# Three blocks of queries projected with tokens in rows and turned by VectorE and DMA, in a two-layer trunk on one Trainium2 core

## The chip, the cores and the metric

The kernel runs on one core of a Trainium2 chip. The metric is device time in microseconds of one execution. Three runs of the kernel before took 975.09, 975.46 and 979.18 us, median 975.46. A profile of one further execution is the source of all durations below. The engines are named as the profile names them: PE is TensorE (matmuls; PEld its weight loads), DVE is VectorE, ACT is ScalarE, POOL is GpSimd, SP is SyncE, which here only issues DMAs.

## The reference, cut to what matters

Two layers, each `h = h + Mixer(RMSNorm(h))`, on 256 tokens with 2048 features. Layer one is a gated DeltaNet with 16 heads of 128; layer two is attention over bands of chunks and takes no part in the change.

```python
def gated_deltanet(h, w_in, conv_w, a_log, dt_bias, out_norm_w, w_out):
    proj = h @ w_in                                # 2048 -> 8224 columns
    qkv = proj[..., :3 * A_INNER]                  # q: columns 0..2047, k, v
    z = proj[..., 3 * A_INNER:4 * A_INNER]
    ...
    qkv = jax.nn.silu(causal_depthwise_conv(qkv, conv_w))   # 4 taps along the tokens
    q = l2_norm(q) * (A_HEAD_DIM ** -0.5)
    k = l2_norm(k)
    ...                                            # decays, triangular solve, scan over 4 chunks
    o = rms_norm(o, out_norm_w) * silu(z)
    return o @ w_out
```

## The kernel before, in words

**Weights and products.** The weights come in a fixed plan of chunks of 512 KB, eight to a block of 512 columns. Each chunk is loaded on SP's queue (L178, tile wt, four buffers), rounded by a ScalarE cast (L204, tile whi) and its rest taken by a VectorE subtract (L205, tile wlo); whi and wlo have three buffers each. Three chunks are fetched ahead of the one in use. The input tokens are split in the same way (tile xb, a high and a low half), and a product is made of three: high by high, high by low, low by high. All big products are matmuls of line L257.

**Three ways to make a block of 512 columns.** "features": features in rows, weights as the stationary side, tokens streamed. "half": the same in halves of 256 columns, in which a weight's high part takes 512 streamed columns (both halves of xb side by side) and its low part 256. Two halves are joined: `joined` copies one part of the accumulator with ScalarE (L327, tile ev, two buffers) and adds the other with VectorE (L328); `scaled` then multiplies by the norm of each token on VectorE (L343, tile raw, one buffer). "tokens": tokens in rows, xb stationary and weights streamed, 96 matmuls of 512 columns. The accumulators of all of them are two buffers of PSUM (tile psp); small products use others (pss). In layer one the first q block is "features", q's other three, k and v are pairs of halves, and the gate z is "tokens".

**Convolution.** `conv` works with features in rows, since the taps shift along the tokens: for each of four groups of 128 features one ScalarE multiply (L546) and three VectorE multiply-adds (L548, tile cv). `q_rest` follows with Silu (L570), Square (L573), two transposes (L579) and a sum (L581); after the last block a small matmul (L587) makes the statistics of all heads.

**What sets the order.** While TensorE goes through a block, `tick` calls `step`, which advances one of several lanes of small work: a lane `landing` first, then bgq and bg2 in turn. q's and k's steps are in bgq in the order of the blocks, the decays of all heads (`decays`, three exponentials per head, L535, one head per chunk from chunk 33 on) in bg2. A lane whose step has to wait for something gives way and nothing behind it in the lane runs. The joining of halves goes ahead of all lanes (`now`). A scheduler then places each engine's instructions in one queue per engine; an instruction that waits holds all behind it on its engine.

**Turning a block by DMA.** Later parts of the kernel already turn tokens-in-rows blocks: `turn_tokens` transposes 32 x 32 squares on VectorE (L438), `trip` stores the tile to DRAM on POOL's queue (L418) and `back` loads it in another order with four DMAs on SP's queue (L424).

Of the kernel before, what the change touches and what calls it, by code (L numbers as in the profile page):

```python
# [10 lines left out]
AF = mybir.ActivationFunctionType  # L11
# [28 lines left out]
def tile_hybrid_trunk(  # L40
# [29 lines left out]
    def slot(tag, kb, dt=F32):  # L70

        return big.tile([P, kb * 256], dt, name=tag, tag=tag)
# [54 lines left out]
    def wide(w, col, c0=0, c1=CPB):  # L127
        return [(w, col, c, 512) for c in range(c0, c1)]
# [4 lines left out]
    def halves(w, col, n):  # L133
        return [x for j in range(n) for x in half(w, col + 256 * j)]


    plan = wide(a_w_in, 0) + halves(a_w_in, 512, 14)
    for col in (6144, 6656, 7168):
        plan += wide(a_w_in, col)
    plan += halves(a_w_in, 4096, 8) + wide(a_w_in, 7680)  # L140
# [198 lines left out]
    def scaled(dst, src, r):  # L339

        if isinstance(src, list):
            for i, ev in enumerate(src):
                dve.tensor_tensor(out=dst[:, 2 * i:2 * i + 2], in0=ev, in1=r.unsqueeze(1).broadcast_to([P, 2, T]),  # L343
                                  op=ALU.mult)
        else:
            dve.tensor_tensor(out=dst, in0=src, in1=r.unsqueeze(1).broadcast_to([P, 4, T]), op=ALU.mult)
# [192 lines left out]
    def conv(src, i0):  # L539

        raw = wk("raw", 1)
        scaled(raw, src, scales["x"][1])
        cv = wk("cv")
        yield cv
        for i in range(4):
            act.activation(out=cv[:, i, :], in_=raw[:, i, :], func=AF.Copy, scale=conv_w(i0 + i, 3))  # L546
            for s in (1, 2, 3):
                dve.scalar_tensor_tensor(out=cv[:, i, s:], in0=raw[:, i, :T - s], scalar=conv_w(i0 + i, 3 - s),  # L548
                                         in1=cv[:, i, s:], op0=ALU.mult, op1=ALU.add)
            yield cv  # L550
# [10 lines left out]
    def q_conv(gi, ps):  # L561
        for cv in conv(ps, 4 * gi):
            yield 1
        qmem[gi] = cv

    def q_rest(gi):
        if gi == 0:
            qmem["q"] = slot("g", 32)[:, :H * T].rearrange("p (h t) -> p h t", h=H)
        q = qmem["q"][:, 4 * gi:4 * gi + 4, :]
        act.activation(out=q, in_=qmem[gi], func=AF.Silu)  # L570
        yield 1
        sq = qmem[gi]
        act.activation(out=sq, in_=q, func=AF.Square)  # L573
        turn = dl[:, 4 * gi:4 * gi + 4, 0, 0:T]
        part = parts[:, 32 * gi:32 * gi + 32]
        yield 1
        for p in range(2):
            hs = slice(2 * p, 2 * p + 2)
            dve.transpose(out=turn[:, hs], in_=sq[:, hs])  # L579
            yield 1  # L580
        dve.reduce_sum(out=part.rearrange("p (h b) -> p h b", h=4), in_=turn.rearrange("p h (b d) -> p h b d", d=32),  # L581
                       axis=AX.X)
        yield 1
        if gi == 3:
            ps = ps_small()
            for c in range(4):
                pe.matmul(ps[32 * c:32 * c + 32, 0:32], lhsT=fold, rhs=parts[:, c:128:4], start=True, stop=True,  # L587
                          tile_position=(0, 32 * c))
            dve.tensor_copy(out=ssq, in_=ps[:, 0:32].rearrange("p (h t) -> p h t", t=2))
            yield 1  # L590
# [370 lines left out]
    for gi in range(4):  # L961
        if gi == 0:
            bgq.append(x_stats())
        ps = pair(xb, 2) if gi else block("features", xb, pre=x_split)
        bgq.append(q_conv(gi, ps))
        if gi == 0:
            bg2.append(decays())
        else:
            if gi == 1:
                bgq.append(q_rest(0))  # L970
            bgq.append(q_rest(gi))
    for gi in range(4):
        bgq.append(k_small(gi, pair(xb)))
    bgq.append(inversion())
# [397 lines left out]
```

## Time and profile before

| what | value |
|---|---|
| median of three runs | 975.46 us (975.09 to 979.18) |
| the profiled execution, its own time | 975.5 us |
| its span, first to last instruction | 973.6 us |
| TensorE busy, share of the span | 966.7 us, 99% |
| VectorE busy | 701.9 us, 72% |
| ScalarE busy | 517.2 us, 53% |
| granted TensorE clock, mean | 1.000 |

A busy time is the time in which an engine works on at least one instruction. In the rows that follow, "out<-in" are the names of the tiles, a size like 128x512 is partitions by elements, and behind "[" or the last "|" stands how long the engine was idle just before and what released it.

### The profile page before, as it was taken

Reading aid. Unit: us, or ns where it says so; the run is one execution under the profiler, and the core shown is the slowest. Engines: PE = TensorE matmul, PEld = TensorE weight load, DVE = VectorE, ACT = ScalarE, POOL = GpSimd, SP = SyncE. Lnnn points to the kernel's source line nnn. Section 1 sums busy time; section 2 is a strip of 40 time slices with the busy share of each in tenths; the row PEclk is TensorE's granted clock in tenths of the full one; section 3 lists DMA queues with packets and bytes.
Section 4 is the critical chain, followed back from the end, with each engine's and each line's share of the span. In section 5 each row is a group of like instructions: output and inputs, shape, how many; then the busy total and the mean of one; then the engine's idle time right before and its main releaser. Section 6 shows DMA issues by size and latency. Waiting matters only on the chain.

```text
span 973.6 us, 14322 instructions
## 1 busy us (share of the span) xinstructions
PE 966.7 (99%) x5291; PEld 821.7 (84%) x5291; DVE 701.9 (72%) x1143; ACT 517.2 (53%) x727; POOL 92.0 (9%) x128
## 2 busy tenths in 40 slices
PE   8999999999999999999999999999999999999998
PEld 7988888888888889888878888888888888888887
DVE  7789787998989877866586655566767676655464
ACT  8465887655547556544365544445454545444332
POOL 1001100122000000101000110111212120000000
PEclk9999999999999999999999999999999999999999
DMA  9657765645665665566978798788798986665695
GB/s 297 195 162 234 233 196 160 179 126 184 173 196 151 180 208 162 169 192 192 304 246 243 223 289 282 215 250 259 235 283 247 278 251 205 202 192 171 206 290 168
DMA packets 142277, 210.01 MB, mean 216 GB/s; under 512 B 10480, under 2 KB 80000, under 8 KB 142208
## 3 DMA queue, kind: packets, MB, share of 16 engines
q1 hardware_dynamic: 136208, 187.33, 64.7%
q0 software_dynamic: 5712, 21.52, 6.1%
q8 instruction: 41, 0.67, 0.3%
q14 instruction: 28, 0.23, 0.1%
q10 hardware_dynamic: 288, 0.26, 0.1%
HBM read 191.76 MB, written 17.32 MB: 215 GB/s over the span
## 4 chain that ended last, share of the span: by engine, by line
PE 93%; DMA 3%; ACT 1%; issue 1%; DVE 1%; SPq 0%; POOL 0%; ACTq 0%; POOLq 0%
PE psp L257 84%; PE pss L631 2%; PE pss L257 1%; PE pss L876 1%; DMA cv<-trip 1%; DMA trip<-cv 1%; PE pss L1159 1%; PE pss L1228 1%; DMA wt<-in_a_w_in_dram 1%; DMA wt<-in_a_w_out_dram 1%; ACT whi L204 0%; DVE wlo L205 0%; PE pss L897 0%; PE pss L898 0%; PE pss L899 0%
## 5 line engine op out<-in xcount | busy, mean ns | idle before, releaser
L205 DVE TENSOR_TENSOR wlo<-wt,whi 128x1024 fp32r<-128x1024 f32 (+2 forms) x324 | 390.0, 1207 | 208.4 <-ACT whi L204 205.0
L204 ACT CAST whi<-wt 128x1024 fp32r<-128x1024 f32 (+2 forms) x324 | 336.5, 1040 | 371.6 <-PE psp L257 288.9
L257 PE MATMUL psp<-whi,xb 128*128 128x512 f32 x1280 | 402.1, 392 | 0.0
L257 PEld LDWEIGHTS psp<-whi,xb 128*128 128x128 f32 x1280 | 240.0, 188 | 49.3
L257 PE MATMUL psp<-wlo,xb 128*128 128x512 f32 x640 | 249.8, 390 | 0.0
L257 PE MATMUL psp<-xb,whi 128*128 128x512 f32 (+1 forms) x832 | 196.2, 376 | 0.9 <-ACT whi L204 0.9
L257 PEld LDWEIGHTS psp<-xb,whi 128*128 128x128 f32 x832 | 148.2, 189 | 25.6 <-ACT whi L204 1.3
L257 PEld LDWEIGHTS psp<-wlo,xb 128*128 128x128 f32 x640 | 120.2, 188 | 24.5
L257 PE MATMUL psp<-whi,g 128*128 128x512 f32 x448 | 138.9, 390 | 0.0
L257 PE MATMUL psp<-xb,wlo 128*128 128x256 f32 x768 | 113.4, 285 | 0.7 <-DVE wlo L205 0.7
L257 PEld LDWEIGHTS psp<-xb,wlo 128*128 128x128 f32 x768 | 103.4, 191 | 5.3 <-DVE wlo L205 1.4
L257 PEld LDWEIGHTS psp<-whi,g 128*128 128x128 f32 x448 | 84.1, 188 | 17.3
L257 PE MATMUL psp<-wlo,g 128*128 128x512 f32 x224 | 87.9, 392 | 0.6 <-DVE wlo L205 0.6
L548 DVE SCALAR_TENSOR_TENSOR cv<-raw,sm,cv 128x255 f32<-128x255 f32 (+2 forms) x144 | 64.2, 479 | 2.4 <-ACT cv L546 2.0
L257 PEld LDWEIGHTS psp<-wlo,g 128*128 128x128 f32 x224 | 42.1, 188 | 10.3 <-DVE wlo L205 2.0
L546 ACT ACTIVATE cv<-raw,sm 128x256 f32<-128x256 f32 x48 | 22.2, 501 | 18.1 <-DVE raw L343 18.1
L418 POOL DMA_DIRECT2D trip<-cv x19 | 10.9, 571 | 190.8 <-DVE cv L438 160.6
L1172 ACT ACTIVATE raw<-raw,mx 128x128 f32<-128x128 f32 (+1 forms) x32 | 14.4, 449 | 16.8 <-DVE mx L1170 16.7
L1115 POOL TENSOR_SCALAR ssn<-ssn,uh 128x4 f32<-128x4 f32 x16 | 12.1, 767 | 68.2 <-DVE ssn L1113 68.2
L635 DVE TENSOR_TENSOR dl<-pss,dl 128x512 f32<-128x512 f32 (+1 forms) x32 | 16.4, 546 | 1.7 <-PE pss L631 1.7
L343 DVE TENSOR_TENSOR raw<-ev,rB 128x512 f32<-128x512 f32 x22 | 14.8, 684 | 2.8 <-DMA trip<-raw 2.8
L328 DVE TENSOR_TENSOR ev<-psp,ev 128x512 f32<-128x512 f32 x23 | 15.7, 682 | 0.1
(247 smaller groups left out, 746.0 us busy)
## 6 DMA issues: line engine op xcount, KB each, us to landing
wt<-in_b_w_in_dram SPq DMA_DIRECT2D x128, 512.0 KB, 4.4
wt<-in_a_w_in_dram SPq DMA_DIRECT2D x125, 512.0 KB, 4.0
wt<-in_a_w_out_dram SPq DMA_DIRECT2D x32, 512.0 KB, 5.2
wt<-in_b_w_out_dram SPq DMA_DIRECT2D x32, 512.0 KB, 4.1
trip<-cv POOLq DMA_DIRECT2D x19, 512.0 KB, 5.5
cv<-trip SPq DMA_DIRECT2D x60, 128.0 KB, 4.5
trip<-dl POOLq DMA_DIRECT2D x8, 384.0 KB, 4.4
tt<-line POOLq DMA_DIRECT2D x4, 512.0 KB, 8.3
```

The costliest lines, as they stand in the source:

```text
L204: cast = act.copy(out=hi[:, js, cs], in_=wt[:, js, cs])
L205: rest = dve.tensor_tensor(out=lo[:, js, cs], in0=wt[:, js, cs], in1=hi[:, js, cs].bitcast(F32), op=ALU.subtract)
L257: state["mm"] = pe.matmul(*args, **kw).ins
L328: dve.tensor_tensor(out=ev, in0=ps[:, :, 0, :], in1=ev, op=ALU.add)
L343: dve.tensor_tensor(out=dst[:, 2 * i:2 * i + 2], in0=ev, in1=r.unsqueeze(1).broadcast_to([P, 2, T]), op=ALU.mult)
L418: nc.gpsimd.dma_start(out=m, in_=u.rearrange("p x c j -> p c (x j)"))
L546: act.activation(out=cv[:, i, :], in_=raw[:, i, :], func=AF.Copy, scale=conv_w(i0 + i, 3))
L548: dve.scalar_tensor_tensor(out=cv[:, i, s:], in0=raw[:, i, :T - s], scalar=conv_w(i0 + i, 3 - s), in1=cv[:, i, s:], op0=ALU.mult, op1=ALU.add)
L631: pe.matmul(dst, lhsT=kq[:, a, i, c:c + P], rhs=rhs, start=(n == 0), stop=(n == 2))
L635: dve.tensor_tensor(out=dl[:, h, :, c], in0=src.rearrange("p (k c) -> p k c", k=2), in1=dec[:, h, c].unsqueeze(1).broadcast_to([P, 2, n]), ...
L1115: pool.tensor_scalar(out=ssn[:, t, :], in0=ssn[:, t, :], scalar1=1.0 / P, scalar2=bmem["uh"][:, t:t + 1], op0=ALU.mult, op1=ALU.add)
L1172: act.activation(out=s[:, a:b], in_=s[:, a:b], func=AF.Exp, bias=mx[:, t:t + 1], accum_out=sums[:, t:t + 1])
```

## The change

q's second to fourth block (columns 512 to 2047) go from pairs of halves to "tokens". The plan of weights has them in whole blocks. `q_turn` evicts each accumulator with two scaled ScalarE activations (the token's norm is now a scale per row), transposes with VectorE and stores; `q_land` loads it back three chunks later and calls it landed five chunks after the store; `q_turned` then puts it in order into raw with one ScalarE copy (L594), convolves and goes on as before. Both are in lanes: the turn and the landing in `landing`, the rest in bgq. The tiles for turning are in the upper half of a slot whose lower half holds q.

```diff
--- before.py
+++ after.py
@@ -134,7 +134,7 @@
         return [x for j in range(n) for x in half(w, col + 256 * j)]
 
 
-    plan = wide(a_w_in, 0) + halves(a_w_in, 512, 14)
+    plan = wide(a_w_in, 0) + wide(a_w_in, 512) + wide(a_w_in, 1024) + wide(a_w_in, 1536) + halves(a_w_in, 2048, 8)
     for col in (6144, 6656, 7168):
         plan += wide(a_w_in, col)
     plan += halves(a_w_in, 4096, 8) + wide(a_w_in, 7680)
@@ -539,7 +539,10 @@
     def conv(src, i0):
 
         raw = wk("raw", 1)
-        scaled(raw, src, scales["x"][1])
+        if callable(src):
+            src(raw)
+        else:
+            scaled(raw, src, scales["x"][1])
         cv = wk("cv")
         yield cv
         for i in range(4):
@@ -563,9 +566,41 @@
             yield 1
         qmem[gi] = cv
 
+    def q_turn(gi, ps):
+        while "s" not in qmem:
+            yield 0
+        n, u, land = (qmem["s"][:, k, :] for k in range(3))
+        n = n.rearrange("p (t d) -> p t d", t=2)
+        u = u.rearrange("p (c x j) -> p x c j", c=4, j=32)
+        for t in range(2):
+            act.activation(out=n[:, t, :], in_=ps[:, t, :], func=AF.Copy, scale=scales["x"][0][:, t:t + 1])
+        yield 1
+        for t in range(2):
+            turn_tokens(u, t, n[:, t, :])
+            yield 1
+        landing.append([q_land(gi, land.rearrange("p (r x j) -> p r x j", r=4, j=32), trip(u), state["use"])])
+
+    def q_land(gi, land, m, end):
+        yield from until(end + 3)
+        back(land, m)
+        yield from until(end + 5)
+        qmem["land", gi] = land
+
+    def q_turned(gi):
+        while ("land", gi) not in qmem:
+            yield 0
+
+        def moved(raw):
+            act.copy(out=raw.rearrange("p h (t r j) -> p (h t) r j", t=2, r=4),
+                     in_=qmem["land", gi].rearrange("p r x j -> p x r j"))
+        yield from q_conv(gi, moved)
+        yield from q_rest(gi)
+
     def q_rest(gi):
         if gi == 0:
-            qmem["q"] = slot("g", 32)[:, :H * T].rearrange("p (h t) -> p h t", h=H)
+            g = slot("g", 32)
+            qmem["q"] = g[:, :H * T].rearrange("p (h t) -> p h t", h=H)
+            qmem["s"] = g[:, H * T:].rearrange("p (n x) -> p n x", n=4)
         q = qmem["q"][:, 4 * gi:4 * gi + 4, :]
         act.activation(out=q, in_=qmem[gi], func=AF.Silu)
         yield 1
@@ -961,14 +996,15 @@
     for gi in range(4):
         if gi == 0:
             bgq.append(x_stats())
-        ps = pair(xb, 2) if gi else block("features", xb, pre=x_split)
-        bgq.append(q_conv(gi, ps))
         if gi == 0:
+            bgq.append(q_conv(0, block("features", xb, pre=x_split)))
             bg2.append(decays())
-        else:
-            if gi == 1:
-                bgq.append(q_rest(0))
-            bgq.append(q_rest(gi))
+            continue
+        ps = block("tokens", xb, 2)
+        if gi == 1:
+            bgq.append(q_rest(0))
+        landing.append([q_turn(gi, ps)])
+        bgq.append(q_turned(gi))
     for gi in range(4):
         bgq.append(k_small(gi, pair(xb)))
     bgq.append(inversion())
```

The lines behind the change stand lower in the changed kernel: L546 becomes L549, L548 L551, L570 L605, L573 L608, L579 L614, L581 L616, L587 L622, L589 L624; lines up to L535 stay.

ScalarE's queue around the first k block, before. The Silu (L570) and Square (L573) are of the last q block, L535 are the decays' exponentials, L327 is the copy of a half.

```order
L327 COPY ev<-psp 128x512
L535 ACTIVATE dl<-dl,ngc 128x128
L535 ACTIVATE dl<-tt,across 128x128
L535 ACTIVATE dl<-dl,ngc 128x128
L570 ACT_TABLE_LOAD
L570 ACTIVATE g<-cv 128x1024
L204 CAST whi<-wt 128x1024
L535 ACT_TABLE_LOAD
L535 ACTIVATE dl<-dl,ngc 128x128
L535 ACTIVATE dl<-tt,across 128x128
L535 ACTIVATE dl<-dl,ngc 128x128
L573 ACTIVATE cv<-g 128x1024
```

The same queue now, from the eviction of the last q block (L576) at the start of the first k block; the first row is the cast at position 4.0 of the prediction's count.

```order
L204 CAST whi<-wt 128x1024 x2
L576 ACTIVATE g<-psp,rx 128x512 x2
L535 ACT_TABLE_LOAD
L535 ACTIVATE dl<-dl,ngc 128x128
L535 ACTIVATE dl<-tt,across 128x128
L535 ACTIVATE dl<-dl,ngc 128x128
L204 CAST whi<-wt 128x1024
L535 ACTIVATE dl<-dl,ngc 128x128
L535 ACTIVATE dl<-tt,across 128x128
L535 ACTIVATE dl<-dl,ngc 128x128 x2
L535 ACTIVATE dl<-tt,across 128x128
L535 ACTIVATE dl<-dl,ngc 128x128
```

And the rows right behind these:

```order
L605 ACT_TABLE_LOAD
L605 ACTIVATE g<-cv 128x1024
L204 CAST whi<-wt 128x1024
L535 ACT_TABLE_LOAD
L535 ACTIVATE dl<-dl,ngc 128x128
L535 ACTIVATE dl<-tt,across 128x128
L535 ACTIVATE dl<-dl,ngc 128x128
L608 ACTIVATE cv<-g 128x1024
L204 CAST whi<-wt 128x1024
```

The first exponentials now stand together with the evictions of the last turned block and with the Silu and Square of the block before it, with three table loads among them.

VectorE's queue around the scaling (L343) of the first k block, before. L328 are the sums of halves, L579 and L581 the last steps of q.

```order
L579 STREAM_TRANSPOSE dl<-cv 128x2x256
L205 TENSOR_TENSOR wlo<-wt,whi 128x1024
L581 TENSOR_REDUCE parts<-dl 128x32
L328 TENSOR_TENSOR ev<-psp,ev 128x512
L205 TENSOR_TENSOR wlo<-wt,whi 128x1024 x2
L343 TENSOR_TENSOR raw<-ev,rB 128x512 x2
L589 COPY ssq<-pss 128x32
L205 TENSOR_TENSOR wlo<-wt,whi 128x1024
L548 SCALAR_TENSOR_TENSOR cv<-raw,sm,cv 128x255
L548 SCALAR_TENSOR_TENSOR cv<-raw,sm,cv 128x254
L548 SCALAR_TENSOR_TENSOR cv<-raw,sm,cv 128x253
L205 TENSOR_TENSOR wlo<-wt,whi 128x1024
```

The same place now:

```order
L614 STREAM_TRANSPOSE dl<-cv 128x2x256
L205 TENSOR_TENSOR wlo<-wt,whi 128x1024
L616 TENSOR_REDUCE parts<-dl 128x32
L205 TENSOR_TENSOR wlo<-wt,whi 128x1024 x2
L343 TENSOR_TENSOR raw<-ev,rB 128x512 x2
L328 TENSOR_TENSOR ev<-psp,ev 128x512 x2
L624 COPY ssq<-pss 128x32
L205 TENSOR_TENSOR wlo<-wt,whi 128x1024
```

Before, the scalings stood ahead of the convolution and of the next block's first sum, with two more subtracts and more work between; now the scalings of the first k block and both sums of the second stand side by side, behind the subtracts.

## The prediction

> **What bounds the kernel now.** I read the page's first and fourth parts, then the table of waits on TensorE.
>
> ```profile
> span 973.6 us, 14322 instructions
> PE 966.7 (99%) x5291; PEld 821.7 (84%) x5291; DVE 701.9 (72%) x1143; ACT 517.2 (53%) x727; POOL 92.0 (9%) x128
> PE 93%; DMA 3%; ACT 1%; issue 1%; DVE 1%; SPq 0%; POOL 0%; ACTq 0%; POOLq 0%
> PE pss L90 <- DVE kT L83: 1.3, 1, 1.3
> PE psp L257 <- DVE wlo L205: 1.2, 4, 0.6
> PE psp L257 <- ACT whi L204: 0.9, 1, 0.9
> ```
>
> TensorE is busy 966.7 of 973.6 us, is 93% of the chain that ended last, and waits 1.3 + 1.2 + 0.9 = 3.4 us in all (us in total, times, longest). So there are two ways for the time to move: the matmuls themselves get cheaper, or one of the helpers comes too late and TensorE stands. Work that VectorE or ScalarE is spared is worth nothing by itself. At most 3.4 us of waits can be removed; nothing bounds how many can be added. The profiled execution took 975.5 us, 1.9 more than its span, and the median of the three runs is 975.46, so the sum is made from 975.5 and stands for the median too.
>
> **Part one, the matmuls.** A position below is a count of blocks of 512 columns of layer one that TensorE has done, taken from the order of its instructions: the q blocks are 0 to 4, the k blocks 4 to 8. This timeline of TensorE (start, busy, engine, line, tile) gives the prices.
>
> ```profile
> 48.24 2.07 PE L257 MATMUL psp<-xb,wlo 128*128 128x256 f32 x16
> 50.15 3.82 PE L257 MATMUL psp<-xb,whi 128*128 128x512 f32 x16
> 53.80 1.11 PE L257 MATMUL psp<-xb,wlo 128*128 128x256 f32 x8
> ```
>
> From start to start, 16 matmuls of 512 columns take 53.80 − 50.15 = 3.65 us, 0.228 each, and 16 of 256 take 50.15 − 48.24 = 1.91, 0.119 each. A q block as two halves is 64 × 0.228 + 64 × 0.119 = 22.2 us. With tokens in rows it is 16 × 2 × 3 = 96 matmuls of 512 columns, 96 × 0.228 = 21.9. The columns are equal (49152); only the overhead of the narrow ones goes. **Three blocks: −1.0 us.**
>
> **Part two, what VectorE and ScalarE are given and spared.** Groups by form (busy us and mean ns of one stand behind the bar, then idle time and its releasers):
>
> ```profile
> L204 ACT CAST whi<-wt 128x1024 fp32r<-128x1024 f32 x317 | 332.7, 1051 | 369.7 <-PE psp L257 288.9 <-issue 24.1 <-DMA wt<-in_a_w_out_dram 14.5
> L327 ACT COPY ev<-psp 128x512 f32<-128x512 f32 x23 | 13.3, 577 | 2.5 <-DVE raw L343 2.5
> L802 ACT ACTIVATE kT<-psp,rx 128x512 f32<-128x512 f32 x8 | 5.0, 681 | 3.5 <-PE pss L631 3.5
> L1141 ACT ACTIVATE dl<-cv,wqk 128x1024 f32<-128x1024 f32 x4 | 4.6, 1154 | 0.0
> L205 DVE TENSOR_TENSOR wlo<-wt,whi 128x1024 fp32r<-128x1024 f32 x317 | 385.8, 1220 | 206.5 <-ACT whi L204 203.1 <-ACT dl L901 2.3
> L328 DVE TENSOR_TENSOR ev<-psp,ev 128x512 f32<-128x512 f32 x23 | 15.7, 682 | 0.1
> L343 DVE TENSOR_TENSOR raw<-ev,rB 128x512 f32<-128x512 f32 x22 | 14.8, 684 | 2.8 <-DMA trip<-raw 2.8
> L438 DVE STREAM_TRANSPOSE cv<-psp 128x512 f32<-128x512 f32 x14 | 9.2, 694 | 3.6 <-DMA trip<-cv 2.6 <-PE psp L257 1.0
> L579 DVE STREAM_TRANSPOSE dl<-cv 128x512 f32<-128x512 f32 x8 | 5.4, 694 | 0.0
> ```
>
> Per block VectorE loses two sums (682 ns) and two scalings (684), 2.7 us, and gains two transposes (694), 1.4. ScalarE loses two copies (577), 1.2 us, and gains two scaled evictions (as L802, 681) and one reordering copy (as L1141, 1154), 2.5. Net −1.3 and +1.4 us in a block of 22 us. I cost this at nothing by itself: TensorE covers it wherever the engine has room. If that cover were gone, the copy (1.15) and the eviction pair would be on the path, 2.5 us a block. The DMA side is one 512 KB store per block on POOL's queue and four 128 KB loads on SP's:
>
> ```profile
> trip<-raw POOLq DMA_DIRECT2D x4, 512.0 KB, 3.6
> cv<-trip SPq DMA_DIRECT2D x16, 128.0 KB, 4.2
> SPq L424 <- DMA trip<-cv: 46.0, 19, 4.8
> ```
>
> The first two are of layer one (300 to 420 us). SP waits at a loading step for its store, up to 4.8 us, and the weight loads of 512 KB queue behind it. The new loads are held back for three chunks (3 × 22 / 8 = 8.3 us) after the store and the copy for two more, 5.6 us, against 3.6 and 4.2: hidden, about zero. If a store is late by the 4.8 us the weights are late by as much, less the two or three chunks that are loaded ahead; I keep 0 to 2.6 us for the copy of the first turned block (position 2.6), which stands ahead of casts on ScalarE. On POOL the stores stand among the masks of the decays, which come long ahead of their exponentials.
>
> **Part three, where the queues now stand.** Q is convolved later, since it has to go out and come back, and all that follows in the same lane goes later with it: q's statistics matmul goes from position 5.4 to 6.1, the first k products from 6.5 to 6.9, the inversion from 12.6 to 13.2. By the end of layer one the order has caught up (the last gated transposes 17.4 before, 17.5 after), and layer two is unchanged. So the lag is not a price; two places in the queues are.
>
> *Place one, the first k block, ScalarE.* The order packs between the casts of positions 4.0 and 4.33 two evictions, a table load, three exponentials, six exponentials, a table load, a Silu, a table load, three exponentials and a Square. The durations from start to start are in one stretch of ScalarE and what follows it on the other two engines:
>
> ```profile
> 148.01 1.05 ACT L204 CAST whi<-wt 128x1024 fp32r<-128x1024 f32 x1 [1.40 <-PE psp L257]
> 148.97 0.58 ACT L327 COPY ev<-psp 128x512 f32<-128x512 f32 x1
> 149.56 1.28 ACT L612 ACT_TABLE_LOAD   x1
> 150.86 1.06 ACT L612 ACTIVATE cv<-cv 128x1024 f32<-128x1024 f32 x1
> 151.92 1.28 ACT L535 ACT_TABLE_LOAD   x1
> 153.22 0.40 ACT L535 ACTIVATE dl<-dl,ngc 128x128 f32<-128x128 f32 x1
> 153.82 0.39 ACT L535 ACTIVATE dl<-dl,ngc 128x128 f32<-128x128 f32 x1
> 154.11 1.03 ACT L204 CAST whi<-wt 128x1024 fp32r<-128x1024 f32 x1
> 155.18 1.23 DVE L205 TENSOR_TENSOR wlo<-wt,whi 128x1024 fp32r<-128x1024 f32 x1 [4.25 <-ACT whi L204]
> 156.46 0.50 PE L257 MATMUL psp<-xb,wlo 128*128 128x256 f32 x2 [0.15 <-DVE wlo L205]
> ```
>
> It is the same mechanism in small: 7.1 us of ScalarE between two casts, the subtract 1.07 after the cast, and TensorE already 0.15 short. Steps: cast 0.96, eviction 0.59, load with its follower's start 1.30, a Silu or Square 1.06, three exponentials 0.89 (153.22 to 154.11), hand-over to another engine 0.04 to 0.05 (155.14 to 155.18, 156.41 to 156.46). After the change, from position 4.0: cast 0.96, two evictions 1.2, load 1.3, exponentials 0.9, cast 0.96, exponentials 1.8, load 1.3, Silu 1.06, cast 1.06, load 1.3, exponentials 0.9, Square 1.06 = 13.8 us. VectorE's two transposes wait for the Square, and the subtract that TensorE needs stands behind them: 2 × 0.69 + 1.22 = 2.6, with hand-overs 16.5. TensorE reaches that weight 5 chunks of 2.78 after position 4.0, at 13.9. **Stall 2.6 us** (0 if the scheduled overlap is better than my sums, 3.2 with the busy means instead of the spacings). What had hidden it before: one group of three exponentials between each two casts.
>
> [...]
>
> *Place two, position 6.0, VectorE.* TensorE's first matmul there writes the accumulator in which the first half of the second k block stood (there are two). It is free once VectorE has made the sum of L328, which needs ScalarE's copy of L327, which needs one of the two buffers ev, which comes free when VectorE has scaled the first k block (L343). Before, these scalings stood at position 5.1, ahead of that half's end. Now they stand behind the subtract of a weight whose cast waits for TensorE to reach the end of 6.0 (three buffers of whi). So at 6.0 TensorE stops, and then follows in a row: cast 1.05, subtract 1.22, two scalings 2 × 0.68 (the copy 0.58 runs beside the second), sum 0.68: 4.3, and five hand-overs of 0.04 to 0.05: **stall 4.5 us**. Queued behind the cast on ScalarE are exponentials and the two copies, behind the scalings on VectorE the sums; all of them only free the path itself. This is a ring of waits and not a matter of load, so I hold it for the surer. Its bounds: 3.4 if TensorE's last matmuls there overlap the cast by a chunk's end, 5.1 with the copy in the row.
>
> *The rest.* The k work is squeezed from positions 5.0 to 9.6 into 6.0 to 9.8, which makes VectorE nearly full there. One window of the trace, inside the k blocks, shows such a state (busy us of PE, PEld, DVE, ACT, POOL; then the granted clock):
>
> ```profile
> 200.00:225.00 25.00, 25.00 (x120) 20.96 (x119) 25.00 (x63) 12.18 (x16) 8.00 (x7) 1.00 0.56 168
> ```
>
> VectorE busy 25.00 of 25 and TensorE still 25.00: fullness alone stopped nothing. Adding up VectorE's instructions by their rows gives about 96 us of work between 6.0 and 10.0, against 105 us of TensorE with its products. So no stall is forced, but local ones can come. Bounds 0 and, for all k blocks, 5 us (two subtracts late by one group of 2.5 each); with the copy of the turned block above (0 to 2.6) I take 0.5, near the row, which shows none.
>
> **Sum:** 975.5 − 1.0 + 2.6 + 4.5 + 0.5 = **982.1 us**, 0.7% slower.
>
> **The rivals.** A measurement of this kernel can tell about 0.5% from no change, that is 970.6 and 980.3.
>
> *Only the matmuls change.* ScalarE and VectorE run ahead at both places, and the ring at 6.0 opens earlier than I read it. For it: TensorE waited only 0.9 + 1.2 us on these helpers in the whole run, through places as dense as 148 to 156. Against it: in the ring no load has to be late. 975.5 − 1.0 = 974.5, no change.
>
> *One of the two stalls is hidden.* With the ring alone, 975.5 − 1.0 + 4.5 = 979.0, and with the smaller losses up to 979.5; with place one alone 977.1. All of it counts as no change.
>
> *VectorE becomes the bound of the k blocks*, or a turned block lands late. Place: 6.0 to 10, where the sums of one half are queued behind products and statistics of the last. It decides once two subtracts come a group late; +5 in place of +0.5: 986.6. For it speaks the 25.00 above, against it the 25.00 of TensorE beside it.
>
> *TensorE runs slower after a stall.* The first nine matmuls of the program, before which it stood still:
>
> ```profile
> 1.25 3.40 PE L90 MATMUL pss<-kT 128*128 128x512 bf16 x9 [1.25 <-DVE kT L83]
> 4.40 0.50 PE L257 MATMUL psp<-xb,whi 128*128 128x256 f32 x2
> ```
>
> Nine of 512 columns take 4.40 − 1.25 = 3.15 us, 0.35 each against 0.228 later: 1.1 us lost after standing, though the column of the granted clock shows 1.00 throughout. If the stall at 6.0 (4.5 us) brings that back, +1.1 once, and at most 2.2 with place one: 983.2 to 984.3. In the trace no later wait is over 0.9 us, so it shows nothing for or against it. [...]
>
> *The change gains.* The saved 1.0 us, and all 2.1 us of waits on casts and subtracts gone with 2.7 us less of VectorE's work a block: 975.5 − 1.0 − 2.1 = 972.4, still within 0.5%. For faster by more, something that I do not see would have to happen.
>
> **How the numbers follow.** Both stalls, about as sized (980 to 985): 0.50. Both and the slow restart: 0.10. Both and a full VectorE: 0.10. One of the two: 0.18. Neither: 0.09. A gain by over 0.5%: 0.03. Slower by over 0.5% are the first three, less 0.04 for the lower edge of the first, 0.66; faster 0.03; no change the remaining 0.31. The range takes in the case of one stall (from 977.1) and the full VectorE (986.6), and leaves out neither stall and what lies above: **977 to 987 us**. The likeliest case's own range is 980 to 985.
>
> **What would show it.** In the profile of the changed kernel the table of waits on TensorE should have a wait of 4 to 5 us at a matmul of L257 whose releaser is VectorE's sum (L328), at about 150 us (position 6.0 is at 148 before: the cast at 148.01 is the one that waits for its end), and one of 2 to 3 us on a subtract (L205), 1.4 blocks or some 31 us before it, in the middle of the first k block. TensorE's busy time should fall by about 1 us. VectorE's should fall by some 4 us (3 × 1.3), ScalarE's rise by about 7 (3 × 1.4 and two more table loads of 1.28). The second half of the span, layer two, should be as long as before. If the ring isn't there (the scalings of the first k block done ahead of 6.0), the step of part three is wrong and the time is below 980. If the waits sum to more than 12 us, the k blocks or the landing were priced too low. If the matmuls that follow the longest wait are slower than 0.24 us each, the restart rival holds.

## The result, and the profile after

The changed kernel takes 987.06 us (986.35 to 987.36), the kernel before 976.08 in the same runs: a ratio of 1.0113, 95% interval 1.0098 to 1.0127. It is slower, as forecast, but by 11.0 us where 6.6 were forecast, just above the upper end of the range (987). The profiled execution took 986.35 us with a span of 984.1, 10.5 more than before.

Two lines of the page of the changed kernel, its waits on TensorE (us in total, times, longest) and two windows (busy us of PE, PEld, DVE, ACT, POOL; granted clock; DMA):

```profile
span 984.1 us, 14150 instructions
PE 970.4 (99%) x5195; PEld 819.7 (83%) x5195; DVE 701.3 (71%) x1137; ACT 525.7 (53%) x732; POOL 93.5 (9%) x131
```

```profile
PE psp L257 <- DVE ev L328: 4.4, 1, 4.4
PE psp L257 <- DVE wlo L205: 3.8, 5, 2.1
PE pss L90 <- DVE kT L83: 1.3, 1, 1.3
PE psp L257 <- ACT whi L204: 0.6, 1, 0.6
PE psp L257 <- ACT g L987: 0.2, 1, 0.2
```

```profile
100.00:125.00 25.00, 21.79 (x110) 18.29 (x109) 16.72 (x25) 23.10 (x40) 0.57 (x1) 0.93 0.76 224
150.00:175.00 25.00, 20.57 (x120) 17.56 (x119) 18.18 (x27) 13.78 (x21) 0.21 (x1) 0.93 0.52 147
```

TensorE waits 10.3 us in place of 3.4. Its busy time rose, though its matmuls have become cheaper, and in just the two windows with long waits the granted clock is 0.93 in place of 1.00. So there are two kinds of loss: waits, and matmuls that run slower behind some of them.

The longest wait is the ring of position 6.0. The timelines of TensorE, ScalarE and VectorE there (start, busy, engine, line, tile):

```profile
151.40 2.00 PE L257 MATMUL psp<-xb,whi 128*128 128x512 f32 x8
157.83 3.42 PE L257 MATMUL psp<-xb,whi 128*128 128x512 f32 x8 [4.43 <-DVE ev L328]
161.18 0.30 PE L622 MATMUL pss<-parts,fold 128*32 128x32 f32 x8
...
153.44 1.04 ACT L204 CAST whi<-wt 128x1024 fp32r<-128x1024 f32 x1 [1.62 <-PE psp L257]
156.38 1.19 ACT L327 COPY ev<-psp 128x512 f32<-128x512 f32 x2 [1.00 <-DVE raw L343]
...
154.51 1.22 DVE L205 TENSOR_TENSOR wlo<-wt,whi 128x1024 fp32r<-128x1024 f32 x1 [1.90 <-ACT whi L204]
155.66 1.28 DVE L343 TENSOR_TENSOR raw<-ev,rB 128x512 f32<-128x512 f32 x2
156.99 1.29 DVE L328 TENSOR_TENSOR ev<-psp,ev 128x512 f32<-128x512 f32 x2
```

The links of the forecast stand in a row: TensorE has done 8 matmuls at 151.40 + 8 × 0.228 = 153.22, then cast, subtract, two scalings, copy and sum, and TensorE goes on at 157.83. Then its 8 matmuls of 512 columns take 161.18 − 157.83 = 3.35 us, 0.42 each in place of 0.228: 1.5 us more.

The other group of waits stands around position 4.1. POOL, VectorE, SP, ScalarE and TensorE:

```profile
80.28 2.17 POOL L518 DMA_DIRECT2D tt<-line  x4 [3.45 <-DMA line<-kT]
90.76 0.58 POOL L418 DMA_DIRECT2D trip<-g  x1
...
83.76 1.28 DVE L438 STREAM_TRANSPOSE g<-g 128x512 f32<-128x512 f32 x2
104.98 2.84 DVE L551 SCALAR_TENSOR_TENSOR cv<-raw,sm,cv 128x255 f32<-128x255 f32 x7
107.74 1.22 DVE L205 TENSOR_TENSOR wlo<-wt,whi 128x1024 fp32r<-128x1024 f32 x1
...
96.67 2.07 SPq L424 DMA_DIRECT2D g<-trip  x4
...
101.81 1.05 ACT L594 COPY raw<-g 128x1024 f32<-128x1024 f32 x1 [6.49 <-DMA g<-trip]
107.21 1.25 ACT L576 ACTIVATE g<-psp,rx 128x512 f32<-128x512 f32 x2
...
109.01 1.68 PE L257 MATMUL psp<-xb,wlo 128*128 128x256 f32 x8 [2.10 <-DVE wlo L205]
110.49 4.98 PE L257 MATMUL psp<-xb,whi 128*128 128x512 f32 x16
115.31 2.08 PE L257 MATMUL psp<-xb,wlo 128*128 128x256 f32 x16
122.52 1.21 PE L257 MATMUL psp<-xb,wlo 128*128 128x256 f32 x8 [0.53 <-DVE wlo L205]
```

The second turned block is transposed by 85.0, but its store leaves POOL only at 90.76, behind the decays' broadcasts and masks; it is loaded back from 96.67 on; ScalarE stands 6.49 us at the copy that puts it in order, with the casts behind it. When it lands, the whole convolution comes at once, seven multiply-adds ahead of the next subtract on VectorE, and TensorE waits 2.10 us for it. The matmuls from 109.01 to 115.31 take 6.30 us in place of 0.95 + 3.65: 1.70 more. The last two rows of ScalarE and TensorE, the evictions of the third turned block and the matmul of the forecast's place one, are used further down.

**The sum of it**, on the span: waits +6.9, slower matmuls 1.70 and 1.63 (the 1.5 above and 0.1 in the next sixteen), +3.3, cheaper matmuls −1.0. That is 9.2 of 10.5. Of the rest about 0.5 us is in how a wait is shown: the start-to-start gap at 157.83 is 4.61 us, the row says 4.43, since a matmul of 512 columns is shown with 0.39 us (99.71 in this profile) while the next starts 0.23 after it. The table has eight waits behind the program's first in place of five; with some 0.16 to 0.18 at each of the three more, that is 0.5. Some 0.8 us stay unexplained. This adds up where TensorE's time went; it does not say what each loss would give back if it were gone (see "Both edits").

### The profile page after: what moved, and what is told of

It is laid out like the page before. It is cut to its first block, busy times and chain, and to the rows that moved or that the text cites. A ratio compares the mean times of both kernels' runs of the same rounds, so it can differ in the third digit from the quotient of the medians.

```text
span 984.1 us, 14150 instructions
## 1 busy us (share of the span) xinstructions
PE 970.4 (99%) x5195; PEld 819.7 (83%) x5195; DVE 701.3 (71%) x1137; ACT 525.7 (53%) x732; POOL 93.5 (9%) x131
## 4 chain that ended last, share of the span: by engine, by line
PE 91%; DVE 3%; ACT 3%; DMA 2%; issue 1%; SPq 1%; ACTq 0%; DVEq 0%
PE psp L257 82%; PE pss L666 2%; DVE wlo L205 1%; DMA trip<-g 1%; DMA g<-trip 1%; PE pss L257 1%; PE pss L911 1%; PE pss L1195 1%; PE pss L1264 1%; DVE cv L551 1%; ACT whi L204 1%; DMA g<-in_xT_dram 1%; ACT L605 0%; PE pss L932 0%; PE pss L933 0%
## 5 line engine op out<-in xcount | busy, mean ns | idle before, releaser
L257 PE MATMUL psp<-whi,xb 128*128 128x512 f32 x1472 | 463.4, 392 | 0.0
L257 PEld LDWEIGHTS psp<-whi,xb 128*128 128x128 f32 x1472 | 276.2, 188 | 56.7
L257 PE MATMUL psp<-wlo,xb 128*128 128x512 f32 x736 | 287.7, 391 | 1.0 <-DVE wlo L205 1.0
L257 PEld LDWEIGHTS psp<-wlo,xb 128*128 128x128 f32 x736 | 138.3, 188 | 29.7 <-DVE wlo L205 1.8
L257 PE MATMUL psp<-xb,whi 128*128 128x512 f32 (+1 forms) x640 | 151.3, 377 | 5.0 <-DVE ev L328 4.4
L257 PEld LDWEIGHTS psp<-xb,whi 128*128 128x128 f32 x640 | 116.4, 194 | 24.8 <-issue 4.8
L257 PE MATMUL psp<-xb,wlo 128*128 128x256 f32 x576 | 88.2, 286 | 3.0 <-DVE wlo L205 2.9
L257 PEld LDWEIGHTS psp<-xb,wlo 128*128 128x128 f32 x576 | 79.0, 192 | 6.6 <-DVE wlo L205 3.8
L551 DVE SCALAR_TENSOR_TENSOR cv<-raw,sm,cv 128x255 f32<-128x255 f32 (+2 forms) x144 | 62.5, 476 | 2.7 <-ACT cv L549 2.5
L549 ACT ACTIVATE cv<-raw,sm 128x256 f32<-128x256 f32 x48 | 21.9, 502 | 7.3 <-DVE raw L343 7.2
L670 DVE TENSOR_TENSOR dl<-pss,dl 128x512 f32<-128x512 f32 (+1 forms) x32 | 16.5, 550 | 1.1 <-PE pss L666 1.1
L1157 DVE TENSOR_TENSOR cv<-psp,rn 128x512 f32<-128x512 f32 x16 | 10.3, 685 | 7.3 <-POOL rn L1153 7.2
L418 POOL DMA_DIRECT2D trip<-dl x8 | 4.4, 546 | 105.8 <-DVE dl L1222 57.7
```

The lines of the kernel that those rows point to most:

```text
L257: state["mm"] = pe.matmul(*args, **kw).ins
L418: nc.gpsimd.dma_start(out=m, in_=u.rearrange("p x c j -> p c (x j)"))
L670: dve.tensor_tensor(out=dl[:, h, :, c], in0=src.rearrange("p (k c) -> p k c", k=2), in1=dec[:, h, c].unsqueeze(1).broadcast_to([P, 2, n]), ...
L1157: dve.tensor_tensor(out=n[:, t, :].rearrange("p (h d) -> p h d", d=P), in0=ps[:, t, :].rearrange("p (h d) -> p h d", d=P), in1=rn[:, t, :] ...
```

## The experiments

All times are medians beside the kernel before on the same chip.

**Store on another queue.** `trip` of the turned blocks on ScalarE's DMA queue.

```diff
-        nc.gpsimd.dma_start(out=m, in_=u.rearrange("p x c j -> p c (x j)"))
+        (q or nc.gpsimd).dma_start(out=m, in_=u.rearrange("p x c j -> p c (x j)"))   # q = nc.scalar for q's blocks
```

> The changed kernel with one edit: the stores of the three turned blocks are issued on ScalarE's DMA queue instead of POOL's, where the second one stood behind the decays' masks. Theory A (the late store is the cause of the first group of waits): the second store leaves some 5 us earlier, the reordering copy no longer waits 6.5 us, the waits of 0.58 and 2.10 us on the cast and the subtract around 103 to 109 us and the slow matmuls after them (1.7 us) go; a part returns as the packed exponentials' stall of up to 2.6 us that was forecast at position 4.6. Time 982.5 to 985.5, against 987.1. Theory B (ScalarE is too full there whatever the store does): the waits stay within 0.5 us and the time within 986 to 988.

988.02 us, ratio 1.0121 (1.0106 to 1.0136): nothing gained. ScalarE's timeline, the landing times of the turned tile's DMAs (of this kernel and then of the changed kernel), and TensorE:

```profile
84.86 0.33 ACTq L418 DMA_DIRECT2D trip<-g  x1
...
101.23 1.05 ACT L594 COPY raw<-g 128x1024 f32<-128x1024 f32 x1 [3.67 <-DMA g<-trip]
```

```profile
DMA to landing us min/median/max: 2.6/4.1/8.8
```

```profile
DMA to landing us min/median/max: 2.9/3.7/5.9
```

```profile
108.44 1.69 PE L257 MATMUL psp<-xb,wlo 128*128 128x256 f32 x8 [2.10 <-DVE wlo L205]
```

The store leaves 5.9 us earlier, but now among the four broadcasts of the decays, and takes up to 8.8 us to land where the longest of the three took 5.9 in the changed kernel (the second of the two lines of landing times); the block arrives 0.6 us earlier than in the changed kernel (101.23 against 101.81), and the wait of 2.10 us is the same. The late store was not the limit by itself. Theory A is refuted as to the cure; B is not shown either, since the copy is still held by its landing.

**No ring.** The first k block's halves are joined into a free part of the turning slot.

```diff
-            ev = work.tile([P, 2, T], F32, name="ev", tag="ev")
+            if spare:      # first k block only
+                ev = qmem["s"][:, 3, 512 * len(dst):512 * len(dst) + 512].rearrange("p (k t) -> p k t", k=2)
+            else:
+                ev = work.tile([P, 2, T], F32, name="ev", tag="ev")
...
```

> The changed kernel with one edit: the two halves of the first k block are joined into a spare part of the turning slot instead of the two ev buffers, so the second k block's copies wait for nothing. Theory A (a ring of waits): the wait of 4.4 us on L328 and the 1.6 us of slow matmuls behind it go: 980.5 to 982. Theory B (the helpers are late in any case there, the ring only names it): a wait of 2 us or more on a cast, subtract or sum stands between positions 6.0 and 7.1 instead, and the time stays above 984.

981.82 us, ratio 1.0061 (1.0041 to 1.0081): 5.2 us of the 6.0 (4.4 and 1.6). No wait on the sum of two halves (L328) is left, and none of 2 us or more between positions 6.0 and 7.1: theory A. What is left on TensorE:

```profile
104.65 3.37 PE L257 MATMUL psp<-xb,whi 128*128 128x512 f32 x8 [2.24 <-ACT whi L204]
...
123.31 1.22 PE L257 MATMUL psp<-xb,wlo 128*128 128x256 f32 x8 [2.12 <-DVE wlo L205]
```

The wait at 123.31 stands 0.625 blocks behind position 4.0, the place one of the forecast. In the whole change it was 0.53 us.

**Both edits.**

> Both edits of the two runs before. If the two groups of waits are independent, the gains add: 976 to 980, with no wait over 2.6 us and a granted clock of 1.00 in all windows. If one feeds the other (a stall gives the helpers time that they then lack), the gain is smaller than the sum of the two by 2 us or more.

981.72 us, ratio 1.0055 (1.0040 to 1.0070), no better than without the ring alone; the store's edit had gained nothing that could be added. TensorE:

```profile
103.58 2.12 PE L257 MATMUL psp<-xb,whi 128*128 128x512 f32 x8 [0.95 <-ACT whi L204]
108.74 1.21 PE L257 MATMUL psp<-xb,wlo 128*128 128x256 f32 x8 [2.09 <-DVE wlo L205]
122.25 1.22 PE L257 MATMUL psp<-xb,wlo 128*128 128x256 f32 x8 [2.13 <-DVE wlo L205]
```

The clock is 1.00 throughout in this execution: behind waits of 2.09 and 2.13 us the matmuls are as fast as ever (1.21 us of eight, as against 1.68 behind the 2.10 above).

The copy of the second block without the ring, and with both edits:

```profile
102.61 1.04 ACT L597 COPY raw<-g 128x1024 f32<-128x1024 f32 x1 [6.20 <-DMA g<-trip]
...
101.54 1.05 ACT L597 COPY raw<-g 128x1024 f32<-128x1024 f32 x1 [3.92 <-DMA g<-trip]
```

From the start of this copy to the matmul at place one it is 122.52 − 101.81 = 20.71 us in the changed kernel, 123.31 − 102.61 = 20.70 without the ring and 122.25 − 101.54 = 20.71 here, although TensorE's waits and slow matmuls on the way differ. So the landing lets ScalarE's queue go, this queue sets when TensorE passes place one, and the losses of TensorE before that only share out a fixed sum. The 1.70 us of slow matmuls of the changed kernel made the next wait 1.6 us shorter (0.53 against 2.13) and cost nothing of their own. The copy came 0.8 us later without the ring than in the changed kernel, which is what the gain of 5.2 falls short of 6.0. The 1.6 us behind the ring are another matter: TensorE has only one wait of 0.2 us after them that could have become shorter.

**Stalls of known length.** The kernel before with a chain between two small matmuls, in layer two, at six places.

```diff
+    def stall(n):
+        with tc.issue_after(state["mm"]):
+            ps = ps_small()
+            first = pe.matmul(ps[:, :P], lhsT=ident, rhs=ident, start=True, stop=True).ins
+        act.copy(out=probe, in_=ps[:, :P])
+        for _ in range(n):
+            pool.tensor_scalar(out=probe, in0=probe, scalar1=1.0, scalar2=None, op0=ALU.mult)
+        ps = ps_small()
+        state["hold"] = pe.matmul(ps[:, :P], lhsT=probe, rhs=ident, start=True, stop=True).ins   # next matmul after it
...
```

> The kernel before with six stalls of different length put into TensorE's queue in layer two, far apart: a small matmul, a ScalarE copy of its result, 2, 4, 7, 10, 14 and 20 POOL operations in a chain on it, and a small matmul that reads the last; the next big matmul comes after it. Theory A (TensorE runs slow for a while after a stall that is long enough): the matmuls behind the short stalls start every 0.228 us as always, those behind the long ones take up to twice that for some 3 us, so that about 1.7 us are lost whatever the length above the bound; the bound is between 0.9 and 4.4 us. Theory B (the slow matmuls of the changed kernel have another cause, such as contention): the spacing behind all six stalls is 0.228 us.

One execution, 1055.54 us. The POOL operations took some 0.53 us each, so the stalls were 3.38 to 18.53 us. The first and the last on TensorE:

```profile
538.00 0.51 PE L274 MATMUL pss<-ident,probe 128*128 128x128 f32 x2 [3.38 <-POOL probe L272]
538.24 0.69 PE L261 MATMUL psp<-whi,xb 128*128 128x512 f32 x1
542.43 0.62 PE L261 MATMUL psp<-whi,xb 128*128 128x512 f32 x2
...
834.54 0.78 PE L261 MATMUL psp<-whi,xb 128*128 128x512 f32 x1
839.08 0.63 PE L261 MATMUL psp<-whi,xb 128*128 128x512 f32 x2
```

Between each pair of rows 11 matmuls start: 4.19 us behind the stall of 3.38 and 4.54 behind that of 18.53, against 11 × 0.228 = 2.51. So 1.7 and 2.0 us are lost, though one stall is five times as long as the other; over all six it is 1.5 to 2.2. All six were followed by slow matmuls. Theory A holds from the shortest of them, 3.38 us, on; no stall here was shorter, so the bound stays open.

**The same with short stalls**, chains of 0 to 9 more ScalarE copies.

```diff
-            pool.tensor_scalar(out=probe, in0=probe, scalar1=1.0, scalar2=None, op0=ALU.mult)
+            act.copy(out=probe, in_=probe)
```

> The kernel before with ten short stalls put into TensorE's queue in layer two, twelve chunks apart: as in the probe before, but the chain is 0 to 9 more ScalarE copies of 128 by 128, some 0.25 to 0.3 us each. Theory A (a stall has to reach a bound): up to some length the matmuls behind a stall start every 0.228 us, above it they are slow for about 3.9 us; the bound lies between 0.9 and 3.4 us. [...]

One execution, 1029.99 us. Three of the ten stalls on TensorE, and the slow matmuls behind one of them:

```profile
608.68 0.49 PE L274 MATMUL pss<-ident,probe 128*128 128x128 f32 x2 [2.90 <-ACT probe L272]
644.11 0.49 PE L274 MATMUL pss<-ident,probe 128*128 128x128 f32 x2 [2.07 <-ACT probe L272]
645.88 1.06 PE L261 MATMUL psp<-whi,xb 128*128 128x512 f32 x2
683.44 0.79 PE L274 MATMUL pss<-ident,probe 128*128 128x128 f32 x2 [4.35 <-ACT probe L272]
```

Behind 1.08, 1.41, 2.77 and 2.90 us nothing was slow; behind 2.07 it was (1.06 us for two matmuls that otherwise show 0.62), and behind the five of 4.12 to 4.79. So length alone does not decide between 2 and 3 us, and theory A does not hold there: no bound on the length was found. The runs with all three blocks turned say the same: waits of 2.10 us were followed by slow matmuls in the changed kernel and not in the last run below.

**One block at a time.** The diff of the first of three; the others have another index.

```diff
-    plan = wide(a_w_in, 0) + wide(a_w_in, 512) + wide(a_w_in, 1024) + wide(a_w_in, 1536) + halves(a_w_in, 2048, 8)
+    plan = wide(a_w_in, 0) + wide(a_w_in, 512) + halves(a_w_in, 1024, 2) + halves(a_w_in, 1536, 2) + halves(a_w_in, 2048, 8)
...
+        if gi not in (1,):
+            bgq.append(q_conv(gi, pair(xb, 2)))     # and q_rest, as before the change
```

> Only the first of the three blocks (columns 512 to 1023) is turned, the other two are pairs of halves as before. In the order of the instructions the scalings of the first k block stand at position 5.1 again, as before the change. Theory A (the losses come from the second block's landing amid the decays' broadcasts and from the ring that the third block makes): 974.5 to 976.5, no wait over 1 us beyond those of before, granted clock 1.00. Theory B (turning a block costs by itself, some 3 to 4 us a block): 978 to 980.

> Only the second block (columns 1024 to 1535) is turned. Theory A: its reordering copy waits for its landing and holds the casts behind it on ScalarE, then its convolution stands in one piece ahead of a subtract: waits of 2 to 3 us between 95 and 112 us, with or without slow matmuls behind them (0 or 1.7 us), 977 to 980.5, and no wait on L328. Theory B (those waits need the other two blocks' work around them too): 974.5 to 976.5.

> Only the third block (columns 1536 to 2047) is turned. In the order of the instructions the scalings of the first k block stand behind the subtracts of position 5.9, as in the whole change. Theory A (the ring belongs to the third block alone): the wait of 4.3 to 4.5 us on L328 and the slow matmuls behind it (1.6 us), 980 to 982. Theory B (the ring closes only where ScalarE and VectorE are late from the earlier blocks): the wait on L328 is under 2 us and the time under 978.5.

| turned | us | ratio, 95% interval | waits on casts, subtracts and sums |
|---|---|---|---|
| first | 980.30 | 1.0044 (1.0027 to 1.0061) | 0.71 and 2.96 on a subtract around 84 to 93 us, small ones |
| second | 979.06 | 1.0031 (1.0018 to 1.0044) | 0.91 on a cast, 0.57, 0.71 and 1.44 on subtracts, 103 to 121 us |
| third | 980.64 | 1.0047 (1.0031 to 1.0062) | 4.43 on L328 at 152 us, 0.8 in all elsewhere |

The third block is the ring, whole and alone (theory A of that run). The second costs 3 us, in the range of its theory A, but in four waits below 1.5 us and not in waits of 2 to 3. The first block alone costs 4 us, where theory A had it for free: so a turned block costs by itself, and the trace shows where. ScalarE and TensorE with the first block alone:

```profile
75.75 1.05 ACT L594 COPY raw<-g 128x1024 f32<-128x1024 f32 x1 [4.61 <-DMA g<-trip]
...
92.53 1.22 PE L257 MATMUL psp<-xb,wlo 128*128 128x256 f32 x8 [2.96 <-DVE wlo L205]
```

The copy stands 4.6 us at the head of ScalarE's queue for its landing; in the run with the second block it is 5.36. The convolution then comes in one piece of eight multiply-adds ahead of a subtract, of nine in the run with the second block.

**First block, landing called later.** The landed tile also moves to another part of the slot.

```diff
-        yield from until(end + 5)
+        yield from until(end + 7)
```

> Only the first block turned, as in the run with the first block alone, and its landing is called landed two chunks later, so that the reordering copy stands two casts further back in ScalarE's queue. Theory A (the copy waits at the head of ScalarE's queue for its landing, 4.6 us, the casts behind it come late, and the convolution then stands in one piece ahead of subtracts): the copy waits under 1 us, the waits of 0.7 and 3.0 us on a subtract go, 975 to 977. Theory B (the convolution of a turned block crowds VectorE wherever it stands, since it meets the next block's): a wait of 2 us or more on a subtract remains and the time is above 978.

981.21 us, ratio 1.0056 (1.0039 to 1.0072), not better than without the edit. ScalarE and TensorE:

```profile
78.56 1.05 ACT L594 COPY raw<-g 128x1024 f32<-128x1024 f32 x1
...
115.60 2.11 PE L257 MATMUL psp<-xb,whi 128*128 128x512 f32 x8 [1.61 <-ACT whi L204]
120.94 1.79 PE L257 MATMUL psp<-xb,wlo 128*128 128x256 f32 x8 [1.83 <-DVE wlo L205]
```

The copy waits no more, and the waits of 0.71 and 2.96 us are gone, as theory A had it. But what stands behind it in the lane is later too, and at 115 to 121 us, among the decays' exponentials, TensorE waits 1.61 and 1.83 us, with slow matmuls behind (1.79). The wait was moved and not removed, and the time is that of theory B.

**Third block, no ring.** The edits of "no ring" and "one block" together.

> Only the third block turned, with the first k block's halves joined into the spare tile. The run with the third block alone lost 4.4 us on the ring and some 1.7 on slow matmuls, and waited 0.8 us elsewhere. If the ring is all that this block costs: 974.3 to 976, within 0.2% of the kernel before, with waits under 1 us in the k blocks. If the decays' exponentials beside it are a cost of their own, as the forecast had it (the wait of 2.1 us on a subtract around 122 us that the two runs without the ring show): 976.5 to 978.

974.33 us against 975.34, ratio 0.9987 (0.9977 to 0.9996). Its waits on TensorE, but for three of 0.2 us:

```profile
PE pss L90 <- DVE kT L83: 1.3, 1, 1.3
PE psp L257 <- ACT whi L204: 0.8, 1, 0.8
```

This is the only one of the kernels that beats both, by 0.1%: the cheaper matmuls of one block (0.3 us) and 0.7 us less of waits than before. It also shows that the loss of the run with the third block alone (4.5 us against the kernel before beside it, where this one gains 1.0) is the ring and what follows it. No wait on a subtract over 0.2 us stands in the first k block here, so the third block's evictions and the exponentials do not make place one by themselves; it takes the late Silu and Square of the second block as well.

**First and third block**, the first landing two chunks later, no ring.

> First and third block turned, the first landing two chunks later, no ring: the two runs beside this one in one kernel. If both work as theory A says, 974 to 976.5, the saving of the matmuls of two blocks being 0.7 us. If the parts disturb each other, 977 to 980.

978.73 us, ratio 1.0034 (1.0024 to 1.0044). Waits of 1.29 on a cast at 99 us and of 1.07 and 1.28 on subtracts at 102 and 110: the parts disturb each other, as the second half of the expectation had it.

**Exponentials later.** Both edits of above, and:

```diff
-DEC0 = 33
+DEC0 = 45
```

> All three blocks turned, stores on ScalarE's queue, no ring, and the decays' exponentials begin 12 chunks later (chunk 45 in place of 33), so that none stands among the evictions, the Silu and the Square of the first k block. Against the run with both edits (981.7): if the packed exponentials are what the wait of 2.13 us at 122 us came from, as the forecast's place one had it, that wait goes and the time is 979 to 980. If it came from the late landing alone, the wait stays and the time is 981 to 982.5; a new wait at the later exponentials would show by its place.

996.33 us, ratio 1.0221 (1.0196 to 1.0246). TensorE:

```profile
108.10 1.22 PE L257 MATMUL psp<-xb,wlo 128*128 128x256 f32 x8 [2.10 <-DVE wlo L205]
...
177.28 3.75 PE L257 MATMUL psp<-xb,whi 128*128 128x512 f32 x8 [4.43 <-DVE ev L331]
```

The wait at 122 us is gone and that at 108 is there still, so the first came from the packed exponentials and the second did not. But a ring of the same length (4.43) has closed one block later, at position 7, with waits on the k products behind it. As a cure it fails; as a test of place one it speaks for the forecast.

## Why the prediction was right or wrong

**The matmuls (−1.0): as forecast** in number and price (5195 instructions in place of 5291), and layer one's waits are where the time went. From about 510 us on TensorE runs 10.75 us behind the kernel before to the end, so layer two is as long as before, as forecast too.

**The ring (4.5): right**, place, links and size: 4.43 us shown, 4.61 from start to start. The runs with the third block alone and without the ring settle that it belongs to that block and to the two buffers ev.

**Place one (2.6): right in size, but it began late.** From the evictions on the chain took 122.52 − 107.21 = 15.3 us, where the forecast's steps give 16.5 − 0.96 = 15.5. The forecast started it with a cast at position 4.0, which TensorE reached at 103.86, so that the evictions would follow at 104.8. They came 2.4 us later. Between position 4.0 and place one TensorE lost 122.52 − 103.86 − 13.9 = 4.8 us: 2.4 of the chain itself and 2.4 of its late start, taken as a wait of 2.10, slow matmuls of 1.70 and a wait of 0.53. With the exponentials elsewhere the wait at place one is gone and the earlier one is not.

**The rest (0.5): the step that failed.** It held the landing for hidden, with the words that the stores "stand among the masks of the decays, which come long ahead of their exponentials". The masks come ahead of the exponentials, but the store comes behind the masks: they wait for the broadcasts (the page's DMA part has 8.2 us from issue to landing), and the store was 5.8 us late (85.0 to 90.76). The forecast asked what waits for the masks and not what waits behind them, and it bounded only the first block's copy, by 2.6 us, not the second's. The other two terms were off as well. The trip was priced at 3.6 + 4.2 = 7.8 us from a quiet stretch; from store to copy it took 101.81 − 90.76 = 11.0, and 101.23 − 84.86 = 16.4 with the store on time but amid the broadcasts. The room was put at 8.3 + 5.6 = 13.9 us; ScalarE stood at the copy 10.3 us behind the transposes (101.81 − 6.49 − 85.0). So it waited 5.8 + 11.0 − 10.3 = 6.5 us. What this cost TensorE is the late start of 2.4 us above and a wait of 0.58 before it. That the landing sets the time of ScalarE's queue here is read from three kernels with the same 20.7 us; that moving such a copy removes the waits behind it was shown for the first block alone; no run cured the second block's. The sign that was set for a landing priced too low, more than 12 us of waits, did not appear (10.3), since part of the loss was slow matmuls.

**The slow restart: a rival of 0.10, and it came about.** It was priced at 1.1 us once, 2.2 twice, and that it stood in no sum is the second reason why the range was missed. It came twice, 1.63 us behind the ring and 1.70 behind the wait of 2.10, but only the first made the kernel longer; without it the time would be an estimated 985.4 (987.06 − 1.63). Its size was nearer than its chance. Both probes and the changed kernel show it; the nine matmuls at the start of the program (0.35 us each) were the only row of before that pointed to it. A wait of 2.10 us sufficed here and one of 2.07 in the probe, while 2.90 did not; what decides between 2 and 3 us was not shown.

**The full VectorE: no.** No wait stands among the k products of the changed kernel after position 6.1, though VectorE is busy 24.77 of 25 us from 200 on. What cost there was VectorE's order, not its load. Its busy time fell by 0.6 us where some 4 were forecast: the groups changed as counted, but the 317 subtracts took 388.6 us in place of 385.8; what is left is not explained. ScalarE's rose by 8.5 (some 7 forecast). One reading of the forecast was off without entering a sum: the two casts of its model stretch stand 154.11 − 148.01 = 6.1 us apart, not 7.1.

**One of the two, neither, a gain: no.** But a small gain was within reach of a part of the change: 0.9987 with the third block alone and no ring.

## What to carry to other kernels

In this kernel, where each engine takes its instructions in the order of its queue, the price of a detour through DRAM was not its work (by the rows of before a gain of 1.3 us on VectorE a block and a loss of 1.4 on ScalarE) but the instruction that waits at the head of a queue for the landing (6.49 us of ScalarE), all that has been queued behind it (a late start of 2.4 us at place one), and the later place in the queues of what it feeds (the ring, 4.43 us). Follow each new DMA from the engine that issues it: what stands ahead of it there (5.8 us on POOL) and what traffic it meets, and price it by rows from such traffic (8.8 us to landing amid the broadcasts, where 3.6 from a quiet stretch was used). A stall of TensorE should be priced with a restart beside it: here slow matmuls came behind every stall from 3.38 us on, with 1.3 to 2.8 us lost in the probes and 1.63 behind the ring, and behind some of 1.83 to 2.24. But where a helper's queue is behind in any case, such a loss only takes the place of the next wait, as 1.70 us of slow matmuls here made it 1.6 shorter; before pricing losses one by one, find the last queue that TensorE has to wait for.

## What the runs showed of the hardware

After every one of the eleven probe stalls of 3.38 to 18.53 us the matmuls of 512 columns started every 0.43 us in place of 0.228, for some 2.5 to 6 us, and 1.3 to 2.8 us were lost (counted as above, from the first big matmul on): 1.5 to 2.2 behind the six long stalls and 1.3 to 2.8 behind the five of 4.1 to 4.8, so no more for a longer one. Of shorter waits some did it (2.07 in the probe, 2.10 in the changed kernel, 2.24 without the ring, 1.83 with the first block landing later) and some did not (2.09 and 2.13 with both edits, 2.10 with the exponentials later, 2.96 with the first block alone, 2.77 and 2.90 in the probe). The granted clock of the windows shows it (0.93 over 25 us in the changed kernel), while the column is 1.00 in the first window (0 to 25 us), where in the profile of before the nine matmuls of the start take 0.35 us each; whether these are the same was not shown.

A 512 KB store that left amid four broadcasts took 8.8 us to land, one that left 5.9 us later 5.9. The loads behind it then took longer as well (a median of 5.9 us in place of 3.7), so that the block arrived only 0.6 us earlier.
